# A hard-max attention kernel: an explicit order for its end phase, multiply-and-sum products, two pick steps at a time, and flag gathers beside value gathers

## Chip, cores and metric

The kernel runs on one core of one Trainium2 chip. The metric is device time in microseconds (us), lower is better. The profile's span, from the first to the last instruction, is about 2 us shorter than that time. Times below are medians of fast runs.

## The reference

For each query row, find the key with the largest dot product and return that key's value row.

```python
B, Sq, Sk, D = 4, 4096, 4096, 128          # q, k, v: float32, normal random
logits = np.matmul(q, k.transpose(0, 2, 1))
best = np.argmax(logits, axis=-1)
return v[b_idx, best, :].astype(np.float32)
```

## The kernel before

The queries form 128 tiles of 128 rows, 32 tiles a batch. The kernel screens keys in groups of four in half precision and repairs doubtful rows later:

- For each tile TensorE and ScalarE build upper bounds of the key groups. VectorE folds them into a table W (`fold`) and takes its eight best entries (`top`, MAX8 into TOP). This is the *screening loop*.
- For each tile GpSimd then fetches the best group's key differences with a *candidate gather* (kg). VectorE computes its half-precision dot products (`dots`), and for every chunk of tiles (8, towards the end 4, 2 and 1) a `pick` chooses the winning key. A *value gather* (vr) for each tile fetches the value rows, and the sync engine stores a chunk of tiles to the output.
- Rows whose decision was too close are *flagged*. For each half of the tiles up to 128 flagged rows are done again exactly: GpSimd gathers their record (FR), query (FQ), three key groups (FK) and, once VectorE has the exact products, the value (FV), and scatters FV over the output.

Picks, dots and the flag work are Python generators. A small scheduler advances them while the loop is written out, so what it decides is the fixed order of instructions on each engine.

```python
# pick (cut): one yield is one step of the scheduler
mx = tensor_reduce(d, max);              yield
lt = tensor_tensor(d, mx, is_lt);        yield
sel = lt * 2**20 + iota;                 yield
wi = tensor_reduce(sel, min);            yield
win = cand * 4 + wi
late_q += [value gather of each tile j] + [store of the chunk];  yield
near = (d + NEAR >= mx);                 yield
CNT = tensor_reduce(near, add)           # input of the flags
# exact (cut): for each of R = 3 key groups, 128 x 512 float32
pr = tensor_tensor(kk[:, r], qq, mult);  yield
d[:, r] = tensor_reduce(pr, add);        yield
# issue (cut), once a tile: one candidate gather, then flag gathers or value gathers
for _ in range(late):                    # late is 1 or 2
    (late_q if late_q and it > T + 1 else fast or late_q).pop(0)()
    while late_q and late_q[0] in stores:
        late_q.pop(0)()
# the loop (cut): loads for the next batch, its key differences, its transposes
if 2 <= qt < 10:    load_part(b + 1, qt - 2)       # keys
elif 10 <= qt < 18: load_part(b + 1, qt - 2)       # queries: natq, on GpSimd
if b + 1 < B and qt >= 13 and qt % 3 == 1:
    unit_q(b + 1, (qt - 13) // 3)                  # TensorE transposes natq
if it % NQT in (9, 13) and it < T:
    put_k(it // NQT + 1, it % NQT // 13)           # k<-kd, a 384 KB write on the sync queue
```

## Time and profile before

| | before |
|---|---|
| time | 494.8 us (494.76 to 495.12) |
| last MAX8 of the screening loop ends | 427.5 us |
| last candidate gather ends | 433.2 us |
| flag indices (rr) ready, FR issued | 445.6, 462.8 us |
| FV issued | 474.7 us |
| scatter issued to end | 477.7 to 478.7 us |
| span | 492.8 us |

The windows of the kernel before show busy time of each engine in three stretches. The columns after the engines are the granted share of the TensorE clock, the DMA share and GB/s:

```profile
core 0: us, PE busy (x) PEld busy (x) DVE busy (x) ACT busy (x) POOL busy (x), PEclk, DMA share, GB/s
40.00:427.00 387.00, 351.42 (x1748) 157.35 (x1746) 381.50 (x714) 364.61 (x460) 254.02 (x274) 1.00 0.38 90
427.00:479.00 52.00, 1.39 (x12) 1.22 (x12) 19.04 (x103) 0.00 (x0) 34.16 (x35) 0.50 0.33 94
479.00:493.00 14.00, 0.00 (x0) 0.00 (x0) 0.00 (x0) 0.00 (x0) 0.00 (x0) 0.50 0.01 4
```

In the first stretch VectorE (DVE) and ScalarE (ACT) are busy nearly all the time. In the second only GpSimd (POOL) works steadily. In the third nothing counts as busy.

The order of time in the tail of the kernel before, cut to the lines that mark it (start, duration, engine, instruction, and in brackets the idle time before it and what ended it):

```profile
426.24 1.22 DVE L229 MAX8 TOP<-W 128x8 f32<-128x1024 f32 x1
...
432.28 0.94 POOL L246 DMA_INDIRECT kg<-k,cand  x1 [0.30 <-DVE near L307]
...
445.40 0.16 DVE L407 SCALAR_TENSOR_TENSOR rr<-rr,rw 128x1 uint32<-128x1 uint32 x1
...
461.57 0.94 POOL L296 DMA_INDIRECT vr<-in_v_dram,win  x1 [0.30 <-issue]
...
462.82 1.01 POOL L411 DMA_INDIRECT FR<-rec,rr  x1 [0.30 <-issue]
464.14 1.00 POOL L411 DMA_INDIRECT FQ<-in_q_dram,row  x1 [0.30 <-issue]
...
465.92 1.00 POOL L411 DMA_INDIRECT FK<-in_k_dram,gb  x1 [0.78 <-DVE gb L425]
...
474.67 1.00 POOL L411 DMA_INDIRECT FV<-in_v_dram,xw_f  x1 [5.15 <-DVE xw_f L460]
477.69 1.02 POOL L433 DMA_INDIRECT out_dram<-FV,row  x1 [2.02 <-DMA FV<-in_v_dram,xw_f]
```

Nearly every value gather takes GpSimd 0.95 us and the next starts 0.30 us later, a pitch of 1.25 us. FR stands behind the last value gather although its index was ready 17 us earlier. Only FK, FV and the scatter wait for data.

Three more engines' lines of the kernel before matter later (I read them only after the result): the sync queue (SPq) near 150 us, the first query load of the next batch, and TensorE's first transpose of it.

```profile
147.57 0.33 SPq L74 DMA_DIRECT2D k<-kd  x1
...
151.85 0.60 POOL L65 DMA_DIRECT2D natq<-in_q_dram  x1
...
153.97 0.33 SPq L300 DMA_DIRECT2D out_dram<-vr  x1
154.41 0.38 SPq L314 DMA_DIRECT2D rec<-TOP  x1
...
154.84 0.29 PE L171 MATMUL uq<-identh,natq 128*128 128x128 f16 x2 [0.89 <-DMA natq<-in_q_dram]
```

The order is put (k<-kd), query load, output store, record write. TensorE waits 0.89 us for the load.

### The profile page before, as it was taken

How to read it: one execution, taken by the hardware profiler on the slowest of the kernel's cores; microseconds unless marked ns; L12 is line 12 of the kernel's file. 1: busy time of each engine (PE TensorE's matmuls, PEld its weight loads, DVE VectorE, ACT ScalarE, POOL GpSimd, SP SyncE). 2: the span in 40 equal slices, each digit the busy share in tenths (PEclk: the TensorE clock that was granted, in tenths of full speed). 3: DMA queues.
4: the chain of work that ended last, by engine and by line, in shares of the span. 5: the costliest groups of instructions: out<-in, count | busy, mean ns of one | idle time of the engine just before them, and what ended most of it. 6: DMA issues, size and time to landing. Idle time of an engine off the chain costs nothing. (4 is left out here: it accounts for less than half of the span.)

```text
span 492.8 us, 6520 instructions
## 1 busy us (share of the span) xinstructions
PE 385.1 (78%) x1960; PEld 174.6 (35%) x1960; DVE 419.6 (85%) x839; ACT 394.8 (80%) x498; POOL 305.7 (62%) x345
## 2 busy tenths in 40 slices
PE   6798999999999999999989989999988999010000
PEld 4344444444444444444444434444333333000000
DVE  3288999999999999999999989999999999781030
ACT  2999999999999999999999989999987999000000
POOL 9125445666788876667888755566646666677720
PEclk9999999999999999999999999999999999655555
DMA  8514452232557542325475412214213222233310
GB/s 141 127 30 83 82 105 57 55 99 55 128 95 167 122 120 57 102 55 124 94 167 122 123 46 86 62 51 124 68 49 92 54 68 85 68 112 112 94 48 0
DMA packets 25128, 43.48 MB, mean 88 GB/s; under 512 B 8040, under 2 KB 16875, under 8 KB 25088
## 3 DMA queue, kind: packets, MB, share of 16 engines
q0 software_dynamic: 18464, 30.97, 30.0%
q1 hardware_dynamic: 6624, 12.06, 6.7%
q8 instruction: 15, 0.25, 0.2%
q14 instruction: 25, 0.20, 0.1%
HBM read 39.59 MB, written 12.19 MB: 105 GB/s over the span
## 5 line engine op out<-in xcount | busy, mean ns | idle before, releaser
L200 ACT ACTIVATE A<-pd 128x1024 f16<-128x1024 f32 x256 | 263.1, 1032 | 12.0 <-PE pd L191 11.4
L246 POOL DMA_INDIRECT kg<-k,cand x128 | 124.3, 971 | 118.6 <-DVE p L265 31.5
L226 DVE TENSOR_TENSOR W<-psn,E 128x1024 int16<-128x1024 f32 x128 | 166.4, 1300 | 20.2 <-ACT E L213 12.4
L191 PE MATMUL psn<-kT,qT 128*128 128x512 f16 x512 | 151.9, 378 | 16.5 <-ACT A L200 10.7
L191 PE MATMUL pd<-kT,qT 128*128 128x512 f16 x512 | 152.2, 379 | 12.1 <-ACT A L200 11.1
L229 DVE MAX8 TOP<-W 128x8 f32<-128x1024 f32 x128 | 156.2, 1220 | 0.0
L210 PE MATMUL psn<-A,identh 128*128 128x512 f16 x512 | 152.1, 378 | 0.0
L296 POOL DMA_INDIRECT vr<-in_v_dram,win x128 | 127.6, 997 | 39.0 <-issue 37.5
L191 PEld LDWEIGHTS <-qT 128*128 128x128 f16 x1024 | 95.9, 97 | 148.5 <-issue 69.3
L213 ACT ACTIVATE E<-psn 128x1024 int16<-128x1024 f32 x128 | 131.0, 1024 | 1.3 <-PE psn L210 1.3
L210 PEld LDWEIGHTS <-identh 128*128 128x128 f16 x512 | 49.7, 97 | 60.8
L261 DVE TENSOR_TENSOR prod<-kg,natq 128x768 f16<-128x768 f16 (+1 forms) x65 | 35.2, 543 | 3.0 <-DMA kg<-k,cand 3.0
L173 ACT ACTIVATE qT<-uq 128x256 f16<-128x256 f32 x60 | 23.7, 394 | 1.1 <-PE uq L171 1.1
L265 DVE TENSOR_TENSOR p<-prod 128x384 f16<-128x384 f16 (+1 forms) x65 | 22.5, 349 | 0.0
L270 DVE TENSOR_REDUCE D<-p 128x6 f32<-128x192 f16 (+1 forms) x65 | 21.6, 334 | 0.0
L166 ACT ACTIVATE kT<-uk 128x256 f16<-128x256 f32 x48 | 18.9, 395 | 0.4 <-PE uk L163 0.4
L171 PE MATMUL uq<-identh,natq 128*128 128x128 f16 x120 | 16.5, 219 | 2.9 <-DMA natq<-in_q_dram 2.9
L351 PE MATMUL fp<-n,tri 128*128 128x1 f32 x4 | 0.9, 304 | 21.2 <-DVE n L343 21.2
L422 DVE TENSOR_SCALAR gi<-FR 128x3 uint32<-128x3 uint32 x2 | 0.3, 159 | 19.7 <-DMA FR<-rec,rr 19.7
L171 PEld LDWEIGHTS <-natq 128*128 128x128 f16 x120 | 11.3, 98 | 16.1 <-DMA natq<-in_q_dram 4.3
L62 POOL DMA_DIRECT2D natk<-in_k_dram x26 | 15.6, 602 | 0.9 <-POOLq L629 0.8
L162 PE MATMUL uk<-identh,natk 128*128 128x128 f16 x96 | 15.8, 219 | 0.0
(99 smaller groups left out, 191.6 us busy)
## 6 DMA issues: line engine op xcount, KB each, us to landing
out_dram<-vr SPq DMA_DIRECT2D x13, 512.0 KB, 2.8
k<-kd SPq DMA_DIRECT2D x8, 384.0 KB, 3.2
natk<-in_k_dram POOLq DMA_DIRECT2D x24, 128.0 KB, 3.8
natq<-in_q_dram POOLq DMA_DIRECT2D x24, 128.0 KB, 3.3
kg<-k,cand POOLq DMA_INDIRECT x128, 2.7
vr<-in_v_dram,win POOLq DMA_INDIRECT x128, 2.6
natk<-in_k_dram POOLq DMA_DIRECT2D x2, 512.0 KB, 5.1
out_dram<-vr SPq DMA_DIRECT2D x4, 256.0 KB, 2.1
```

Of the source, the lines that this page charges most:

```text
L171: nc.tensor.matmul(out=ps[:, i * P:(i + 1) * P], lhsT=natq[b % 2][:, g * 2 + i, :], rhs=identh, start=True, stop=True)
L173: nc.scalar.activation(out=qT[b % 2][:, g * 256:(g + 1) * 256], in_=ps, func=AF.Copy, scale=QSCALE)
L191: nc.tensor.matmul(out=ps[:, n * 512:(n + 1) * 512], lhsT=qT[b % 2][:, qt * P:(qt + 1) * P], rhs=kT[b % 2][:, u * 1024 + n * 512:u * 1024 ...
L200: nc.scalar.activation(out=A, in_=ps, func=AF.Abs)
L210: nc.tensor.matmul(out=ps[:, n * 512:(n + 1) * 512], lhsT=identh, rhs=A[:, n * 512:(n + 1) * 512], start=False, stop=True)
L213: nc.scalar.activation(out=E, in_=ps, func=AF.Relu)
L226: nc.vector.tensor_tensor(out=W_t[t % NW].bitcast(I16)[:, 1::2], in0=ps, in1=E, op=OP.max)
L229: nc.vector.max(out=TOP[:, t, :], in_=W_t[t % NW].bitcast(FP32))
L246: near_q.append(lambda j=j: nc.gpsimd.indirect_dma_start(out=kg[:, j].rearrange("p f d -> p (f d)"), out_offset=None, in_=k16[t0 // NQT], ...
L261: nc.vector.tensor_tensor(out=prod, in0=kg, in1=natq[b % 2][:, x - b * NQT:x - b * NQT + m, :].unsqueeze(2).to_broadcast([P, m, 3, P]), op ...
L265: nc.vector.tensor_tensor(out=p1, in0=prod[:, :, :, 0:64], in1=prod[:, :, :, 64:128], op=OP.add)
L296: late_q.append(lambda j=j: nc.gpsimd.indirect_dma_start(out=vr[:, j, :], out_offset=None, in_=v_flat, in_offset=IOA(ap=win[:, j:j + 1], a ...
```

## The change

Its intent: order the end phase by hand, so that the flag work of the second half starts early and its waits are filled with value gathers; compute the exact products with a multiply-and-sum instruction; stop flag gathers from displacing value gathers in the loop; and get winners, hence value gathers, earlier by taking two pick steps at a time.

```diff
 # pick: near and CNT come first
+        near = ...; yield
+        CNT = tensor_reduce(near, add); yield "cnt"
         lt = ...
 # exact
-            tensor_tensor(pr, kk[:, r], qq, mult)      # 128 x 512
-            tensor_reduce(d[:, r, :], pr, add)
+            for f in range(4):                         # 128 x 128
+                tensor_tensor_reduce(out=pr, in0=kk[:, r, f * P:(f + 1) * P], in1=qq,
+                                     op0=mult, op1=add, accum_out=d[:, r, f:f + 1])
 # chunks of tiles
-    cuts = list(range(0, T - 24 + 1, 8)) + [T - x for x in (20, 16, 12, 8, 6, 4, 2, 1, 0)]
+    cuts = list(range(0, T - 16 + 1, 8)) + [T - x for x in (12, 8, 4, 0)]
 # step: two pick steps at a time
-                else:
-                    moved |= advance(s, it, free)
+            elif advance(s, it, False) and s["kind"] == "pick" and s in live:
+                advance(s, it, False)
 # issue: a flag gather is added to the value gather
+        if fast and it >= rest[0]:
+            fast.pop(0)()
+            rest[0] = it + 3
+        take_late(2 if n == 0 and len(late_q) > 4 else 1)
 # end phase (new function flags_last, cut)
+        late(LATE)                                     # ten value gathers
+        get(FR, rec, rr); get(FQ, q_flat, row)
+        late(1)
+        for r in range(3): get(FK[:, r], k4, gb[:, r])
+        late(3)
+        win = whole(exact(FK, FQ, gb, 3, "fe"))
+        get(FV, v_flat, win)
+        late(1 << 20)                                  # the rest
+        scatter FV to out                              # waits for all stores
 ... (the loop rewritten for it in range(T), then an explicit drain of dots and picks)
```

More of the change, by code (lines that the diff above doesn't have):

```diff
@@ L23 @@
 NEAR = 0.5
+LATE = 10
 @with_exitstack
@@ L251, in gather @@
         near_q.append(mark)
-        start(dots(c, t0, n), "dots")
+        start(dots(c, t0, n), "dots", c)
     def dots(c, x, m):
@@ L281, in pick @@
         yield "dve",
+        near = sp.tile([P, n, 4], FP32, tag=f"near{n}", name=f"near_{c}")
+        nc.vector.scalar_tensor_tensor(out=near, in0=d, scalar=NEAR, in1=mx.to_broadcast([P, n, 4]),
+                                       op0=OP.add, op1=OP.is_ge)
+        yield "dve",
+        nc.vector.tensor_reduce(out=CNT[:, t0:t1], in_=near, axis=AX_X, op=OP.add)
+        done.add(("cnt", c))
+        yield "cnt",
         lt = sp.tile([P, n, 4], FP32, tag=f"lt{n}", name=f"lt_{c}")
@@ L293, in pick @@
         nc.vector.scalar_tensor_tensor(out=win, in0=cand, scalar=4.0, in1=wi, op0=OP.mult, op1=OP.add)
-        vr = rp.tile([P, n, P], FP32, tag=f"vr{n}", name=f"vr_{c}", bufs=3)
+        vr = rp.tile([P, n, P], FP32, tag=f"vr{n}", name=f"vr_{c}", bufs=3 if n == 8 else 4)
         for j in range(n):
@@ L304, in pick @@
         late_q.append(store)
-        yield "dve",
-        near = sp.tile([P, n, 4], FP32, tag=f"near{n}", name=f"near_{c}")
-        nc.vector.scalar_tensor_tensor(out=near, in0=d, scalar=NEAR, in1=mx.to_broadcast([P, n, 4]),
-                                       op0=OP.add, op1=OP.is_ge)
-        yield "dve",
-        nc.vector.tensor_reduce(out=CNT[:, t0:t1], in_=near, axis=AX_X, op=OP.add)
-        done.add(("cnt", c))
     def put_rec(t0, t1):
@@ L435, in flag_segment, with flags_first @@
         yield "until", lambda: not fast, 0
+    LF = {}
+    def flags_first(t0, t1):
+        S = t1 - t0
+        H = LF["H"] = fp.tile([P, S, 4], U32, tag="H", name="H_e")
+        nc.vector.tensor_scalar(out=H, in0=TOP.bitcast(U32)[:, t0:t1, 0:4], scalar1=16, scalar2=None,
+                                op0=OP.logical_shift_right)
+        F = LF["F"] = fp.tile([P, S], FP32, tag="F", name="F_e")
+        nc.vector.scalar_tensor_tensor(out=F, in0=H[:, :, 1], scalar=TAU, in1=H[:, :, 0], op0=OP.add, op1=OP.is_ge)
@@ new lines, in flags_last, with get @@
+    def flags_last(t0, t1, win_last, late):
+        S = t1 - t0
+        H, F = LF["H"], LF["F"]
+        nc.vector.scalar_tensor_tensor(out=F, in0=CNT[:, t0:t1], scalar=1.5, in1=F, op0=OP.is_gt, op1=OP.max)
+        Ec = fp.tile([P, S], FP32, tag="Ec", name="Ec_e")
+        nc.vector.tensor_tensor(out=Ec, in0=F, in1=codes[:, t0:t1], op=OP.mult)
+        e8 = fp.tile([P, 8], FP32, tag="e8", name="e8_e")
+        nc.vector.max(out=e8, in_=Ec)
+        val = fp.tile([P, 8], FP32, tag="val", name="val_e")
+        nc.vector.tensor_scalar(out=val, in0=e8, scalar1=0.5, scalar2=None, op0=OP.is_gt)
+        n2 = fp.tile([P, 3], FP32, tag="n2", name="n2_e")
+        nc.vector.tensor_reduce(out=n2[:, 0:1], in_=val, axis=AX_X, op=OP.add)
+        ps = pp.tile([P, 1024], FP32, tag="u", name="fp_e")
+        nc.tensor.matmul(out=ps[:, 0:1], lhsT=tri, rhs=n2[:, 0:1], start=True, stop=True)
+        win_last()
+        bs = fp.tile([P, 1], FP32, tag="bs", name="bs_e")
+        nc.vector.tensor_copy(out=bs, in_=ps[:, 0:1])
+        posn = fp.tile([P, 8], FP32, tag="posne", name="posn_e")
+        nc.vector.scalar_tensor_tensor(out=posn, in0=iota_r[:, 0:8], scalar=bs, in1=val, op0=OP.add, op1=OP.mult)
+        rec2 = fp.tile([P, 8, 2], BF16, tag="rec2", name="rec2_e")
+        nc.vector.tensor_copy(out=rec2[:, :, 0], in_=e8)
+        nc.vector.tensor_copy(out=rec2[:, :, 1], in_=iota_p.to_broadcast([P, 8]))
+        OH = fp.tile([P, 8, P], BF16, tag="OH", name="OH_e")
+        for z in range(8):
+            nc.vector.tensor_scalar(out=OH[:, z], in0=iota_h, scalar1=posn[:, z:z + 1], scalar2=None, op0=OP.is_equal)
+        ps2 = pp.tile([P, 1024], FP32, tag="u", name="fq_e")
+        for s in range(8):
+            nc.tensor.matmul(out=ps2[:, 0:2], lhsT=OH[:, s, :], rhs=rec2[:, s, :], start=s == 0, stop=s == 7)
+        nc.vector.tensor_reduce(out=n2[:, 1:2], in_=F, axis=AX_X, op=OP.add)
+        tp = fp.tile([P, 2], FP32, tag="tp", name="tp_e")
+        nc.vector.tensor_copy(out=tp, in_=ps2[:, 0:2])
+        rw = fp.tile([P, 2], FP32, tag="rw", name="rw_e")
+        nc.vector.tensor_scalar(out=rw[:, 0:1], in0=tp[:, 0:1], scalar1=0.5, scalar2=float(1 << 20), op0=OP.is_lt, op1=OP.mult)
+        rr = fp.tile([P, 1], U32, tag="rr", name="rr_e")
+        nc.vector.scalar_tensor_tensor(out=rr, in0=tp[:, 1:2], scalar=float(T), in1=tp[:, 0:1], op0=OP.mult, op1=OP.add)
+        nc.vector.scalar_tensor_tensor(out=rr, in0=rr, scalar=-1.0, in1=rw[:, 0:1], op0=OP.add, op1=OP.add)
+        tb = fp.tile([P, 2], U32, tag="tb", name="tb_e")
+        nc.vector.tensor_scalar(out=tb[:, 0:1], in0=tp[:, 0:1], scalar1=-1.0, scalar2=0.0, op0=OP.add, op1=OP.max)
+        nc.vector.scalar_tensor_tensor(out=rw[:, 1:2], in0=tp[:, 1:2], scalar=float(NQT), in1=tp[:, 0:1], op0=OP.mult, op1=OP.add)
+        nc.vector.tensor_scalar(out=tb[:, 1:2], in0=tb[:, 0:1], scalar1=NQT.bit_length() - 1, scalar2=None,
+                                op0=OP.logical_shift_right)
+        nc.vector.scalar_tensor_tensor(out=rw[:, 1:2], in0=tb[:, 1:2], scalar=float(Sq - NQT), in1=rw[:, 1:2], op0=OP.mult, op1=OP.add)
+        row = fp.tile([P, 1], U32, tag="row", name="row_e")
+        nc.vector.scalar_tensor_tensor(out=row, in0=rw[:, 1:2], scalar=-1.0, in1=rw[:, 0:1], op0=OP.add, op1=OP.add)
+        def get(dst, src, idx, hi):
+            nc.gpsimd.indirect_dma_start(out=dst, out_offset=None, in_=src, in_offset=IOA(ap=idx, axis=0),
+                                         bounds_check=hi - 1, oob_is_err=False)
+        late(LATE)
+        get(FR, rec, rr, P * T)
+        get(FQ, q_flat, row, P * T)
+        late(1)
+        bo = fp.tile([P, 1], U32, tag="bo", name="bo_e")
+        nc.vector.tensor_scalar(out=bo, in0=row, scalar1=Sq.bit_length() - 1, scalar2=NG.bit_length() - 1,
+                                op0=OP.logical_shift_right, op1=OP.logical_shift_left)
+        F4 = fp.tile([P, S], FP32, tag="F4", name="F4_e")
+        nc.vector.scalar_tensor_tensor(out=F4, in0=H[:, :, 3], scalar=TAU, in1=H[:, :, 0], op0=OP.add, op1=OP.is_ge)
+        nc.vector.tensor_reduce(out=n2[:, 2:3], in_=F4, axis=AX_X, op=OP.add)
+        nc.tensor.matmul(out=ps[:, 512:515], lhsT=ones, rhs=n2, start=True, stop=True)
+        gi = fp.tile([P, 3], U32, tag="gi", name="gi_e")
+        nc.vector.tensor_scalar(out=gi, in0=FR[:, 0:3], scalar1=NG - 1, scalar2=NG - 1, op0=OP.bitwise_and, op1=OP.bitwise_xor)
+        gb = fp.tile([P, 3], U32, tag="gb", name="gb_e")
+        nc.vector.tensor_tensor(out=gb, in0=gi, in1=bo.to_broadcast([P, 3]), op=OP.add)
+        for r in range(3):
+            get(FK[:, r, :], k4, gb[:, r:r + 1], B * NG)
+        tot = fp.tile([P, 3], FP32, tag="tot", name="tot_e")
+        nc.vector.tensor_copy(out=tot, in_=ps[:, 512:515])
+        hd = fp.tile([P, 2], FP32, tag="hd", name="hd_e")
+        nc.vector.tensor_scalar(out=hd[:, 0:1], in0=tot[:, 1:2], scalar1=-float(P), scalar2=0.0, op0=OP.add, op1=OP.max)
+        nc.vector.tensor_tensor(out=hd[:, 1:2], in0=tot[:, 1:2], in1=tot[:, 0:1], op=OP.subtract)
+        for a in (hd[:, 0:1], hd[:, 1:2], tot[:, 2:3]):
+            nc.vector.tensor_tensor(out=HARD, in0=HARD, in1=a, op=OP.add)
+        late(3)
+        win = whole(exact(FK, FQ, gb, 3, "fe"))
+        get(FV, v_flat, win, B * Sk)
+        late(1 << 20)
+        nc.gpsimd.indirect_dma_start(out=out_flat, out_offset=IOA(ap=row, axis=0), in_=FV, in_offset=None,
+                                     bounds_check=P * T - 1, oob_is_err=False)
@@ L439, in exact @@
         for r in range(R):
-            pr = fp.tile([P, 4, P], FP32, tag="xp", name=f"xp_{name}_{r}")
-            nc.vector.tensor_tensor(out=pr, in0=kk[:, r, :].rearrange("p (f d) -> p f d", f=4),
-                                    in1=qq.unsqueeze(1).to_broadcast([P, 4, P]), op=OP.mult)
-            yield "dve", 0.7
-            nc.vector.tensor_reduce(out=d[:, r, :], in_=pr, axis=AX_X, op=OP.add)
-            yield "dve", 0.7
+            for f in range(4):
+                pr = fp.tile([P, P], FP32, tag="xp", name=f"xp_{name}_{r}_{f}", bufs=2)
+                nc.vector.tensor_tensor_reduce(out=pr, in0=kk[:, r, f * P:(f + 1) * P], in1=qq, scale=1.0, scalar=0.0,
+                                               op0=OP.mult, op1=OP.add, accum_out=d[:, r, f:f + 1])
+                yield "dve", 0.2
         ix = fp.tile([P, R, 4], FP32, tag=f"xi{R}", name=f"xi_{name}")
@@ L508, with start @@
     live = []
-    def start(g, kind):
-        live.append({"g": g, "kind": kind, "wake": 0, "until": None, "n": 0})
+    def start(g, kind, c=None):
+        live.append({"g": g, "kind": kind, "c": c, "wake": 0, "until": None, "n": 0})
     def ready(s, it):
@@ L533, in advance @@
         return True
-    def step(it, free=False):
-        moved = True
-        while moved:
-            moved = False
-            waiting = [s for s in live if s["kind"] == "dots" and ready(s, it)]
-            quota = 2 if len(waiting) > 1 or free else 1
-            for s in list(live):
-                if s["kind"] == "dots":
-                    if quota and advance(s, it, free):
-                        quota -= 1
-                        moved = True
-                else:
-                    moved |= advance(s, it, free)
-            if not free:
-                return
@@ L551, in issue @@
-    def issue(it):
-        if it > T + 1:
-            while near_q:
-                near_q.pop(0)()
-            late = 2
-        else:
-            n = 0
-            while near_q and (n < 1 or near_q[0] in marks):
-                g = near_q.pop(0)
-                n += g not in marks
-                g()
-            late = 2 if n == 0 and len(late_q) + len(fast) > 4 else 1
-        for _ in range(late):
-            if fast or late_q:
-                (late_q if late_q and it > T + 1 else fast or late_q).pop(0)()
-            while late_q and late_q[0] in stores:
-                late_q.pop(0)()
@@ L569, with step @@
-    it = 0
-    while it < T + 2 or live or fast or near_q or late_q:
-        if it <= T:
-            b, qt = it // NQT, it % NQT
-            if 2 <= qt < 10:
-                load_part(b + 1, qt - 2)
-            elif 10 <= qt < 18:
-                load_part(b + 1, qt - 2)
-            if b + 1 < B and qt >= 8 and (qt - 8) % 3 < 2:
-                unit_k(b + 1, (qt - 8) // 3 * 2 + (qt - 8) % 3)
-            if b + 1 < B and qt >= 13 and qt % 3 == 1:
-                unit_q(b + 1, (qt - 13) // 3)
-            if 0 < it < 13:
-                unit_q(0, it + 3)
-            elif 0 < b < B and qt < 9:
-                unit_q(b, qt + 7)
-            if it > 0:
-                screen(it)
-        if 0 <= it - 1 < T:
+    def step(it):
+        waiting = [s for s in live if s["kind"] == "dots" and ready(s, it)]
+        quota = 2 if len(waiting) > 1 else 1
+        for s in list(live):
+            if s["kind"] == "dots":
+                if quota and advance(s, it, False):
+                    quota -= 1
+            elif advance(s, it, False) and s["kind"] == "pick" and s in live:
+                advance(s, it, False)
@@ new lines, with take_late @@
+    rest = [0]
+    def take_late(n):
+        while n > 0 and late_q:
+            g = late_q.pop(0)
+            n -= g not in stores
+            g()
+        while late_q and late_q[0] in stores:
+            late_q.pop(0)()
+    def issue(it):
+        n = 0
+        while near_q and (n < 1 or near_q[0] in marks):
+            g = near_q.pop(0)
+            n += g not in marks
+            g()
+        if fast and it >= rest[0]:
+            fast.pop(0)()
+            rest[0] = it + 3
+        take_late(2 if n == 0 and len(late_q) > 4 else 1)
@@ new lines, in gathers @@
+    def gathers(t):
+        for c, (t0, t1) in enumerate(chunks):
+            if t0 <= t < t1 and ((t - t0) % 2 or t == t1 - 1):
+                x = t0 + (t - t0) // 2 * 2
+                gather(c, x, t - x + 1)
+            if t == t0:
+                start(pick(c, t0, t1), "pick", c)
+        if t % 8 == 7:
+            put_rec(t - 7, t + 1)
+        if t == SEGS[1] - 1:
+            last = [c for c, x in enumerate(chunks) if x[1] == t + 1][0]
+            start(flag_segment(0, t + 1, lambda: ("cnt", last) in done, lambda: ("out", last) in done), "flags")
@@ new lines @@
+    for it in range(T):
+        b, qt = it // NQT, it % NQT
+        if 2 <= qt < 10:
+            load_part(b + 1, qt - 2)
+        elif 10 <= qt < 18:
+            load_part(b + 1, qt - 2)
+        if b + 1 < B and qt >= 8 and (qt - 8) % 3 < 2:
+            unit_k(b + 1, (qt - 8) // 3 * 2 + (qt - 8) % 3)
+        if b + 1 < B and qt >= 13 and qt % 3 == 1:
+            unit_q(b + 1, (qt - 13) // 3)
+        if 0 < it < 13:
+            unit_q(0, it + 3)
+        elif 0 < b < B and qt < 9:
+            unit_q(b, qt + 7)
+        if it > 0:
+            screen(it)
+        if it >= 1:
@@ L588 @@
             fold(it - 1)
-        if it % NQT in (9, 13) and it < T:
+        if it % NQT in (9, 13):
             put_k(it // NQT + 1, it % NQT // 13)
-        step(it, it >= T + 2)
-        if 0 <= it - 2 < T:
+        step(it)
+        if it >= 2:
             top(it - 2)
-        for t in ([it - 3] if it < T else [it - 3, it - 2] if it == T else [it - 2]):
-            if not 0 <= t < T:
-                continue
-            for c, (t0, t1) in enumerate(chunks):
-                if t0 <= t < t1 and ((t - t0) % 2 or t == t1 - 1):
-                    x = t0 + (t - t0) // 2 * 2
-                    gather(c, x, t - x + 1)
-                if t == t0:
-                    start(pick(c, t0, t1), "pick")
-            if t % 8 == 7:
-                put_rec(t - 7, t + 1)
-            for t0, t1 in zip(SEGS[:-1], SEGS[1:]):
-                if t == t1 - 1:
-                    last = [c for c, x in enumerate(chunks) if x[1] == t1][0]
-                    start(flag_segment(t0, t1, lambda last=last: ("cnt", last) in done,
-                                       lambda last=last: ("out", last) in done), "flags")
@@ L610, with flush, drain @@
-        step(it, it >= T + 2)
-        issue(it)
-        it += 1
+        if it >= 3:
+            gathers(it - 3)
+        step(it)
+        issue(it)
+    def flush():
+        while near_q:
+            near_q.pop(0)()
+    screen(T)
+    gathers(T - 3)
+    flush()
+    top(T - 2)
+    fold(T - 1)
+    top(T - 1)
+    gathers(T - 2)
+    gathers(T - 1)
+    flush()
+    assert not [s for s in live if s["kind"] == "flags"] and not fast
+    def drain(group, stop=None):
+        while group:
+            for s in list(group):
+                try:
+                    y = next(s["g"])
+                except StopIteration:
+                    group.remove(s)
+                    live.remove(s)
+                    continue
+                if y[0] == "until":
+                    assert y[1]()
+                if y[0] == stop:
+                    return
@@ L613 @@
+    for p in [s for s in live if s["kind"] == "pick"]:
+        c = p["c"]
+        dot = [s for s in live if s["kind"] == "dots" and s["c"] == c]
+        while dot:
+            two, dot = dot[:2], dot[2:]
+            drain(two)
+        last = c == len(chunks) - 1
+        if last:
+            flags_first(T // 2, T)
+        drain([p], "cnt" if last else None)
+    flags_last(T // 2, T, lambda: drain([p]), take_late)
     man.__exit__(None, None, None)
```

## The prediction

> **What bounds the kernel now.** The table of windows shows two phases. From 40 to 427 us VectorE is busy 94 to 100% (100% from 350 on), ScalarE nearly as much: the screening loop, about 3.02 us a query tile. From 427 on all matrix work is over, yet the span ends at 492.8. The order of time shows GpSimd alone there: after the last candidate gather (ends 433.2) it issues 23 value gathers at a pitch of 1.25 us, then FR, FQ, three FK, FV and the scatter, which ends at 478.7. Only the last seven wait: FK 0.8 us for the group numbers, FV 5.2 for the exact products, the scatter 2.0 for FV. The flag indices (rr, row) were ready at 445.6, yet FR came at 462.8: 17 us behind value gathers. From the scatter to the span's end are 14.1 us (the queue records show a GpSimd drain of 9.1); I take them as fixed.
>
> **What the change does.** GpSimd issues 322 transfers before and after. But in the loop flag gathers no longer displace value gathers, and the last chunks have 4 tiles instead of 2, 2, 1, 1, so 24 transfers (17 value, 7 flag) follow the last candidate gather, not 30: 6 x 1.25 = 7.5 us less. FR and FQ go after ten value gathers, FK one later, FV after three more, three are left behind FV: the waits of 0.8, 5.2 and 2.0 us are filled, some 7 us less. The last two candidate gathers go back to back, about 2 us sooner. New: the last store (128x512, 2.1 us to landing) comes after the last value gather and the scatter waits for it: about 4 us.
>
> Products: six 128x512 VectorE instructions of 0.69 us (4.4 us in the tail) become twelve multiply-and-sums of 128x128. The Trainium skill (VectorE: DVE Perf Modes, section "Two Vector instructions with no wait between them") says that an op that writes its accumulator out is two instructions; the build shows 24. Estimate from the trace (512 elements 0.69, one element 0.15 us, pitch 0.08 under the duration): 0.28 to 0.4 us a pair, about even in the loop; only the last group's four pairs, 1.2 us, follow the last FK landing.
>
> Cost: two pick steps at a time put dependent small instructions side by side (mx then near, sel then wi). Dependent neighbours in the tail have a pitch of 0.19 us, independent ones 0.07: 0.12 x 2 x 15 chunks, up to 3.6 us in a loop that VectorE bounds. Against it, about 1.8 us of picks and dots move behind the last top-8. Net: last top-8 at about 429, 1.4 us later.
>
> **Sum.** Candidate gathers end at 431.5, FR issues at 444 (rr just in time), FV at 456, the last value gather ends at 461, its store lands at 465, the scatter ends at 466: 12.5 us sooner. 494.8 - 12.5 = 482.3 us; range 479.5 to 485.5. Chances: faster 0.85, within 2% 0.14, slower 0.01.
>
> **What would show it.** Last candidate gather to scatter about 34 us, GpSimd idle little beyond its 0.3 us issue gaps, but for about 4 us before the scatter, released by the last store; no wait over 1 us before FV; the last top-8 ending between 428 and 430; 14 us after the scatter.
>
> **What would make it wrong.** Vector work after the last top-8 (8 tiles of dots, two picks, the flags) outlasting the ten gathers before FR, so FR stalls the queue; accumulator pairs of 0.5 us or more; dependent neighbours costing nothing, or more; three transfers in one tile delaying candidate gathers; a longer drain.

## The result

| | before | predicted | after |
|---|---|---|---|
| time, us | 494.8 | 482.3 (479.5 to 485.5) | 489.06 (488.84 to 489.34) |
| last MAX8 ends | 427.5 | 429 | 434.2 |
| last candidate gather ends | 433.2 | 431.5 | 437.6 |
| FR issued | 462.8 | 444 | 450.4 |
| FV issued | 474.7 | 456 | 462.6 |
| last value gather ends | 462.5 | 461 | 467.3 |
| scatter ends | 478.7 | 466 | 472.9 |
| scatter's end to end of span | 14.1 | 14.1 | 14.1 |

The ratio of after to before is 0.9883 (95% interval 0.9866 to 0.99): faster, but by less than 2%. Ratios here are the mean time of one kernel's fast runs over that of the other's of the same rounds, so not quite the ratio of the medians that I quote.

The windows of the changed kernel, cut at its own last MAX8 and at its scatter's end:

```profile
core 0: us, PE busy (x) PEld busy (x) DVE busy (x) ACT busy (x) POOL busy (x), PEclk, DMA share, GB/s
40.00:434.00 394.00, 354.51 (x1749) 158.34 (x1747) 382.35 (x718) 365.49 (x460) 259.37 (x282) 0.99 0.36 91
434.00:473.00 39.00, 2.28 (x12) 1.74 (x12) 18.58 (x109) 0.00 (x0) 26.30 (x27) 0.50 0.31 98
473.00:487.00 14.00, 0.00 (x0) 0.00 (x0) 0.00 (x0) 0.00 (x0) 0.00 (x0) 0.50 0.01 4
```

The second stretch shrank from 52 to 39 us, but the first grew from 387 to 394 us with no more VectorE work in it (381.5 and 382.4 us busy).

The tail of the changed kernel in the order of time:

```profile
432.93 1.23 DVE L230 MAX8 TOP<-W 128x8 f32<-128x1024 f32 x1
...
436.52 1.04 POOL L247 DMA_INDIRECT kg<-k,cand  x1 [0.30 <-issue]
...
447.41 0.16 DVE L483 SCALAR_TENSOR_TENSOR rr_e<-rr_e,rw_e 128x1 uint32<-128x1 uint32 x1
...
450.43 1.01 POOL L494 DMA_INDIRECT FR<-rec,rr_e  x1 [0.31 <-issue]
...
454.31 1.00 POOL L494 DMA_INDIRECT FK<-in_k_dram,gb_e  x1 [0.30 <-DVE HARD L520]
...
462.55 1.00 POOL L494 DMA_INDIRECT FV<-in_v_dram,xw_fe  x1 [0.67 <-DVE xw_fe L550]
```

Its last three lines, from a later window that shows the last store by itself:

```profile
466.35 0.94 POOL L304 DMA_INDIRECT vr<-in_v_dram,win  x1 [0.30 <-issue]
468.88 0.33 SPq L308 DMA_DIRECT2D out_dram<-vr  x1
471.86 1.01 POOL L525 DMA_INDIRECT out_dram<-FV,row_e  x1 [4.57 <-SPq L567]
```

FR follows its index (rr) after 2.9 us. FV waits 0.67 us. The scatter waits 4.57 us; the last store was issued 3.0 us before it. All this is near the forecast, only some 6 us late. So the loss is in the loop. Comparing the start of each MAX8 in the two traces shows where: at tile 42 the changed kernel is 0.4 us behind, at tile 43 it is 3.5 us behind, at tile 70 still 4.1, at tile 78 8.9 us, and 8.1 us at tile 124. (Parts of the jump near 78 are the first half's flag work, which stands at other tiles in the two kernels.)

The same engines near 150 us as shown of the kernel before:

```profile
151.10 0.33 SPq L308 DMA_DIRECT2D out_dram<-vr  x1
151.53 0.38 SPq L75 DMA_DIRECT2D k<-kd  x1
152.01 0.80 SPq L315 DMA_DIRECT2D rec<-TOP  x1
152.42 0.60 POOL L66 DMA_DIRECT2D natq<-in_q_dram  x1
...
157.24 0.28 PE L172 MATMUL uq<-identh,natq 128*128 128x128 f16 x2 [2.69 <-DMA natq<-in_q_dram]
```

The store is 2.9 us earlier and the put 4.0 us later, so that store, put and record write all go out within 1 us just ahead of the query load. TensorE now waits 2.69 us for the load. Then something else shows, in the windows of the changed kernel around that wait:

```profile
core 0: us, PE busy (x) PEld busy (x) DVE busy (x) ACT busy (x) POOL busy (x), PEclk, DMA share, GB/s
150.00:157.00 7.00, 4.04 (x21) 1.72 (x19) 7.00 (x11) 4.84 (x6) 5.77 (x7) 1.00 0.82 220
157.00:161.00 4.00, 3.76 (x12) 1.40 (x13) 1.91 (x5) 2.51 (x4) 3.09 (x5) 0.58 0.57 104
```

The same two windows of the kernel before:

```profile
150.00:157.00 7.00, 6.03 (x33) 2.65 (x31) 7.00 (x15) 6.36 (x9) 5.65 (x7) 1.00 0.76 168
157.00:161.00 4.00, 3.90 (x25) 1.90 (x24) 4.00 (x8) 4.00 (x6) 3.21 (x4) 1.00 0.72 129
```

From 157 to 161 us the granted clock is 0.58: the clock record has it halved from 157.6 us for 3.4 us, and again from 260.0 us for 3.4 us behind a wait of 2.77 us for the next batch's first query load. Before, it is 1.00 up to the end of the loop; VectorE is busy for all of the 4 us there, in the changed kernel for 1.91 of them.

Two pick steps at a time are why the store comes early: the winners of this chunk are known at 124.0 us instead of 124.8, so its first value gather still catches the slot at 124.8 (128.0 before), its eighth goes out at 147.5 instead of 150.8, and the store behind them comes as much sooner. The put stands behind the store in the sync queue, and so waits for the store's gathers although its data are there (VectorE finished kd at 148.0, the put went out at 151.5).

The Trainium skill (DMA: Bandwidth & Descriptors, section "Issuing engines are not separate DMA queues") says that transfers started by scalar, sync and GpSimd run on the same 16 DMA engines and interleave. The packet records agree that the engines are shared: in the kernel before the packets of that query load (1,024 bytes) start about 1.2 us after its issue; in the changed kernel they start about 2.3 us after it, behind the 4,096-byte packets of the store and most of the 3,072-byte packets of the put. They show little interleaving: the store's packets start from 151.9 to 153.6 us, the put's from 153.2, the load's from 154.7, mostly in the order of issue.

### The profile page after: what moved, and what is told of

Read it like the earlier page. It is cut to its first block, busy times and chain, and to the rows that moved or that the text cites. A ratio compares the mean times of both kernels' runs of the same rounds, so it can differ in the third digit from the quotient of the medians.

```text
span 487.0 us, 6530 instructions
## 1 busy us (share of the span) xinstructions
PE 389.1 (80%) x1960; PEld 176.1 (36%) x1960; DVE 421.0 (86%) x849; ACT 395.5 (81%) x498; POOL 302.3 (62%) x345
## 5 line engine op out<-in xcount | busy, mean ns | idle before, releaser
L192 PE MATMUL psn<-kT,qT 128*128 128x512 f16 x512 | 153.0, 380 | 18.0 <-ACT A L201 12.1
L211 PE MATMUL psn<-A,identh 128*128 128x512 f16 x512 | 153.0, 380 | 0.0
L304 POOL DMA_INDIRECT vr<-in_v_dram,win x128 | 124.1, 970 | 39.3 <-issue 35.6
L214 ACT ACTIVATE E<-psn 128x1024 int16<-128x1024 f32 x128 | 131.1, 1024 | 3.5 <-PE psn L211 3.5
L262 DVE TENSOR_TENSOR prod<-kg,natq 128x768 f16<-128x768 f16 x64 | 35.0, 549 | 0.0
L266 DVE TENSOR_TENSOR p<-prod 128x384 f16<-128x384 f16 x64 | 22.3, 351 | 0.0
L271 DVE TENSOR_REDUCE D<-p 128x6 f32<-128x192 f16 x64 | 21.5, 339 | 0.0
L269 DVE TENSOR_TENSOR p<-p 128x192 f16<-128x192 f16 x64 | 15.7, 248 | 0.0
L66 POOL DMA_DIRECT2D natq<-in_q_dram x26 | 15.5, 596 | 0.0
## 6 DMA issues: line engine op xcount, KB each, us to landing
natk<-in_k_dram POOLq DMA_DIRECT2D x24, 128.0 KB, 3.6
natq<-in_q_dram POOLq DMA_DIRECT2D x24, 128.0 KB, 3.1
```

Of the source, the lines that this page charges most:

```text
L192: nc.tensor.matmul(out=ps[:, n * 512:(n + 1) * 512], lhsT=qT[b % 2][:, qt * P:(qt + 1) * P], rhs=kT[b % 2][:, u * 1024 + n * 512:u * 1024 ...
L211: nc.tensor.matmul(out=ps[:, n * 512:(n + 1) * 512], lhsT=identh, rhs=A[:, n * 512:(n + 1) * 512], start=False, stop=True)
L214: nc.scalar.activation(out=E, in_=ps, func=AF.Relu)
L262: nc.vector.tensor_tensor(out=prod, in0=kg, in1=natq[b % 2][:, x - b * NQT:x - b * NQT + m, :].unsqueeze(2).to_broadcast([P, m, 3, P]), op ...
L266: nc.vector.tensor_tensor(out=p1, in0=prod[:, :, :, 0:64], in1=prod[:, :, :, 64:128], op=OP.add)
L304: late_q.append(lambda j=j: nc.gpsimd.indirect_dma_start(out=vr[:, j, :], out_offset=None, in_=v_flat, in_offset=IOA(ap=win[:, j:j + 1], a ...
```

## The experiments

Theory T: the pick change moves transfers so that the query load comes late, TensorE idles, and its clock is halved. Rival R: two dependent small instructions side by side cost VectorE time in every chunk. Rival F: flag gathers on top of value gathers overload GpSimd in the loop. The kernel before took 495.0 to 495.3 us beside all runs but two (d1_extra and b2_put_late, told last). The changed kernel was measured in other rounds, beside 494.8, so a difference to its 489.06 is uncertain by some 0.4 us.

### One pick step at a time (a1_single)

```diff
-            elif advance(s, it, False) and s["kind"] == "pick" and s in live:
-                advance(s, it, False)
+            else:
+                advance(s, it, False)
```

> The changed kernel with one pick step at a time again (as before), all else kept. Theory T (store order): two pick steps move an output store ahead of the k-difference put in the sync queue; store, put and record write then go out together with the first query load of the next batch, TensorE idles 2.7 us at its transposes twice, and its clock is halved for 3.4 us after each. T expects: in the sync queue the put comes before the store again, no TensorE wait over 1 us at those transposes, no clock drop before the loop ends, last top-8 ending at 427 to 429 instead of 434, time 482.5 to 485. Rival R (dependent neighbours cost VectorE about 0.12 us twice a chunk) also expects less, at most 3.6 us (485.5), gained evenly over the chunks. Rival F (flag gathers added to value gathers overload GpSimd) expects about 489.

483.39 us (ratio to before 0.9763, 0.9746 to 0.9779). Put, load, store are in the old order (147.6, 151.9, 156.7 us), no clock drop in the loop, the last MAX8 ends at 425.9 us, even earlier than I expected. The wait at the first transpose was 1.37 us, over the 1 us I had given. 26 transfers instead of 24 follow the last candidate gather. The loss comes with the pick change, but this run alone cannot tell T from R.

### The put one tile earlier (a2_put_early)

```diff
-        if it % NQT in (9, 13):
-            put_k(it // NQT + 1, it % NQT // 13)
+        if it % NQT in (8, 12):
+            put_k(it // NQT + 1, it % NQT // 12)
```

> The changed kernel with the two k-difference puts a batch one tile earlier, so that they stand before the output store in the sync queue; pick steps still two at a time. T expects the wait at the transposes to shrink below 1.5 us and no clock drop, 483 to 486 (the output store itself still falls near the query load). R and F expect no change, 488.5 to 489.5.

484.93 us (0.9789, 0.9772 to 0.9805). R and F fall short here: the picks are still double and the flag gathers still added. But the waits are 2.25 and 1.88 us, not below 1.5: the put was a small part of the delay. The clock was not halved at all. With no put ahead of it, the load's packets still start 2.4 us after its issue, behind the store's.

Why a wait of 2.25 us kept the clock where one of 2.69 lost it, can be worked out from the traces. Within each trace the changes of the clock record lie whole multiples of 3.41 us apart. Cut each trace into these steps, and add up in each the time in which TensorE neither multiplies nor loads weights. In all 14 traces, every one of the 1,699 full-clock steps with at most 1.88 us of such idle time was followed by a step at full clock, and each of the 24 with 1.91 us or more by one at half. The wait of 2.69 us lies in one step; a boundary cuts that of 2.25 us into 1.53 and 0.72 us. So the length of a wait alone does not decide; where it falls in the steps does too, and the steps lie differently in every run.

### The first transpose one tile later (a3_uq_late)

```diff
-        if b + 1 < B and qt >= 13 and qt % 3 == 1:
+        if b + 1 < B and (qt == 14 or qt >= 16 and qt % 3 == 1):
```

> The changed kernel with only the first query transpose of a batch moved one tile later, puts and stores as they are. T expects the collision of transfers to stay but TensorE not to wait for it: no wait over 1 us there, no clock drop, last top-8 ending at 427.5 to 429.5, time 482.5 to 484.5. R and F expect 488.5 to 489.5.

482.66 us (0.975, 0.9733 to 0.9766), as T expects. The waits are 0.51 us each, for ScalarE and not for the load; no clock drop, the last MAX8 ends at 427.8 us. Transfers stand as in the changed kernel; only TensorE's demand moved. The 6.4 us that separate this from 489.06 are what the two late loads cost.

### The pick change alone, in the kernel before (b1_double)

```diff
-                    moved |= advance(s, it, free)
+                    went = advance(s, it, free)
+                    moved |= went
+                    if went and not free and s["kind"] == "pick" and s in live:
+                        advance(s, it, free)
```

> The kernel before with the pick change alone (two steps at a time in the loop). T expects the same swap in the sync queue as in the changed kernel, waits of over 2 us at the transposes and clock drops near 157 and 260 us, and 498 to 502. R expects at most 3.6 us more, 496 to 498.5, spread evenly and without a clock drop. F expects 494.8.

502.4 us (1.0148, 1.0117 to 1.0179), so 7 us slower than before and 0.4 over T's range. Waits of 2.37 and 2.32 us; the clock was halved behind the first (156.9 us, for 3.4 us), not behind the second, which a step boundary cuts into 1.73 and 0.59 us. Of the two drops that I expected one came. The pick change by itself, without any of its partners, brings the loss. Not all of it is the two late loads: against the kernel before, MAX8 starts 4.3 us late at tile 66, after the first of them, 6.9 at tile 90, after the second, and 8.8 at the last tile. The last 1.9 us come where no late load stands; R may claim them (no run tests that by itself).

### Idle matmuls in front of the transpose (c1_filler)

```diff
+        if b > 0 and g == 0:
+            for i in range(8):
+                nc.tensor.matmul(out=ps, lhsT=wz[:, 0:P], rhs=wz[:, 0:256], start=True, stop=True)
```

> The changed kernel with eight idle matmuls of 256 columns put in front of each batch's first query transpose (their result is overwritten), so that TensorE is idle for a shorter time while it waits for the same late load; nothing moves in the transfer queues. Theory T2: about half of each loss is the halved clock[...] (drops seen behind 2.37, 2.69 and 2.77 us, none behind 2.25 and 2.32). T2 expects idle times below 2 us, no clock drop before the loop ends, and 485.5 to 487.5. Rival: the clock drop costs nothing because ScalarE and VectorE bind, the loss is the wait alone; 488.8 to 489.5.

486.52 us (0.9835, 0.9813 to 0.9856); the four runs are 485.55, 485.79, 487.25 and 487.88. In the profiled run TensorE's lines at the same place show the fillers, and then the transpose at nearly the same time as in the changed kernel (157.52 and 157.24 us), behind a shorter wait:

```profile
154.87 1.03 PE L173 MATMUL uq<-wz 128*128 128x256 f16 x8
157.52 0.28 PE L175 MATMUL uq<-identh,natq 128*128 128x128 f16 x2 [1.62 <-DMA natq<-in_q_dram]
```

Its windows show the clock at 1.00 where the changed kernel had 0.58:

```profile
core 0: us, PE busy (x) PEld busy (x) DVE busy (x) ACT busy (x) POOL busy (x), PEclk, DMA share, GB/s
150.00:157.00 7.00, 5.39 (x31) 2.69 (x29) 7.00 (x13) 5.27 (x7) 5.52 (x7) 1.00 0.85 222
157.00:161.00 4.00, 3.48 (x20) 1.71 (x21) 2.82 (x6) 3.05 (x4) 3.39 (x4) 1.00 0.61 107
```

There is no drop in its whole loop, and its last MAX8 ends 3.7 us earlier than in the changed kernel. The rival, a halved clock that costs nothing (488.8 to 489.5 us), falls. Of the 6.3 us by which a3_uq_late's last MAX8 is earlier, then, 3.7 us are the halved clock and the other 2.6 us the waits themselves, if the fillers cost nothing. This split rests on one profiled run, the fastest. The second idle time is 2.22 us, not below 2 as expected, but a step boundary cuts it in this run into 1.2 and 1.0 us. In the two runs that are 1.5 to 2.3 us slower the steps may have fallen otherwise and a drop have come; they were not profiled, so this is not shown.

### The old products (c2_old_products)

```diff
 # on a3_uq_late: exact() as in the kernel before
```

> The changed kernel with the late first query transpose (a3_uq_late, 482.66) and with the products of before (six 128x512 multiply or reduce instructions). In the traces a multiply-and-sum with its accumulator read has a pitch of 0.21 us (twelve: 2.5 us), an old instruction 0.6 in the loop (six: 3.7 us) and 0.72 in the tail (4.4 us). Expected: last top-8 1.2 us later than in a3_uq_late, the wait before FV from 1.0 to about 2 us, time 484 to 485.5. If the new products gain nothing: 482.7.

484.87 us (0.979, 0.9774 to 0.9806): 2.2 us more than a3_uq_late, as expected. The last MAX8 ends 1.05 us later and the wait before FV is 2.14 instead of 0.95 us. The new products in the tail of the changed kernel look like this:

```profile
457.73 0.29 DVE L533 CUSTOM_DVE_ANT_0 xp_fe<-FK,FQ 128x128 f32<-128x128 f32 x1 [3.19 <-DMA FK<-in_k_dram,gb_e]
457.95 0.08 DVE L533 DVE_READ_ACCUMULATOR2_ANT xd_fe<- 128x1 f32 x1
457.95 0.28 DVE L533 CUSTOM_DVE_ANT_0 xp_fe<-FK,FQ 128x128 f32<-128x128 f32 x1
458.16 0.08 DVE L533 DVE_READ_ACCUMULATOR2_ANT xd_fe<- 128x1 f32 x1
```

A pair of multiply-and-sum and accumulator read has a pitch of 0.21 us, below my estimate of 0.28 to 0.4.

### Flag gathers displacing value gathers again (c3_displace)

```diff
 # on a3_uq_late, in issue() (cut: the lines that these replace):
+        room = 2 if n == 0 and len(late_q) + len(fast) > 4 else 1
+        while fast and room:
+            fast.pop(0)()
+            room -= 1
+        take_late(room)
```

> a3_uq_late (482.66) with the first half's flag gathers displacing value gathers again, as before. The built order then has 31 transfers behind the last candidate gather instead of 24, the seven more all value gathers behind FV. Expected 7 x 1.25 = 8.75 us more, 490.5 to 492; the end of the loop unchanged within 0.5 us. If the extra transfers in the loop cost time there (rival F), the loop ends earlier by 1 us or more and the sum is below 490.

491.08 us (0.9917, 0.9901 to 0.9934): 8.4 us more than a3_uq_late for seven more transfers in the tail, 1.2 us each; expected were 8.75. The last MAX8 ends at 427.6 us against 427.8: the added transfers cost the loop nothing. F is out.

### All value gathers ahead of FV (c4_tail)

```diff
 # on a3_uq_late
-        late(3)
         win = whole(exact(FK, FQ, gb, 3, "fe"))
-        get(FV, v_flat, win, B * Sk)
         late(1 << 20)
+        get(FV, v_flat, win, B * Sk)
```

> a3_uq_late (482.66) with all value gathers issued before FV, so that the last store runs while FV lands. Expected: the gap before the scatter from 4.5 to about 2 us, no wait before FV, 480 to 481. If the scatter's wait is not for the last store: 482.7.

481.45 us (0.9719, 0.9703 to 0.9735). FV does not wait, but the gap before the scatter is 3.98 us, not 2:

```profile
458.43 0.94 POOL L304 DMA_INDIRECT vr<-in_v_dram,win  x1 [0.30 <-issue]
459.68 1.01 POOL L494 DMA_INDIRECT FV<-in_v_dram,xw_fe  x1 [0.30 <-DVEq L566]
...
464.67 1.01 POOL L524 DMA_INDIRECT out_dram<-FV,row_e  x1 [3.98 <-SPq L566]
```

From the end of the last value gather to the scatter are 5.3 us (4.5 in a3_uq_late): its landing, the store and the store's landing are one chain, and the landing of FV hides only part of it. The gain is 1.2 us instead of about 2, and the time lies 0.45 us over the 480 to 481 expected. This version beats both kernels.

### The query loads one tile earlier (e1_load_first)

```diff
-        elif 10 <= qt < 18:
-            load_part(b + 1, qt - 2)
+        if 9 <= qt < 17:
+            load_part(b + 1, qt - 1)
```

> The changed kernel with the query loads of the next batch issued one tile earlier, so that the first of them is issued about 2.5 us sooner, ahead of the output store that the change moved in front of it; the transposes stay where they are. Theory T, as sharpened by the put runs (what counts is whether the 512 KB output store goes out before or behind the first query load; the put adds little): no wait over 1.4 us at the first transposes, no clock drop before the loop ends, 482.5 to 484.5. If the late load has another cause than the store in front of it, 487 to 489.

482.62 us (0.9751, 0.9735 to 0.9767), as T expects. The load now goes out ahead of the store:

```profile
149.25 0.64 POOL L66 DMA_DIRECT2D natq<-in_q_dram  x1
...
150.92 0.33 SPq L308 DMA_DIRECT2D out_dram<-vr  x1
151.35 0.38 SPq L75 DMA_DIRECT2D k<-kd  x1
151.83 0.50 SPq L315 DMA_DIRECT2D rec<-TOP  x1
```

TensorE's trace has no wait over 0.3 us at these transposes and no clock drop. Together with a3_uq_late this settles the cause: it is enough to move either the load or its use by a tile.

### The put one tile later, in the kernel before (b2_put_late)

```diff
-        if it % NQT in (9, 13) and it < T:
-            put_k(it // NQT + 1, it % NQT // 13)
+        if it % NQT in (10, 14) and it < T:
+            put_k(it // NQT + 1, it % NQT // 14)
```

> The kernel before with the k-difference puts one tile later and nothing else: in the built sync queue the output store now stands ahead of the put, as in the changed kernel, but pick steps stay single and no dependent instructions are neighbours. T (the order of store and put, and the late query load that follows) expects waits of over 1.5 us at the first query transpose of batches 2 and 3, [...]and 497 to 501. R (dependent neighbours) expects 494.8 to 495.5.

507.7 us, on a chip where the kernel before took 505 to 512 us (0.997, 0.9894 to 1.0046): the time decides nothing. The trace does: the store was ahead of the put, but the query load (151.4 us) was ahead of both (153.0 and 153.4), and the waits were 0.58 and 0.50 us. My expectation was wrong: the order of store and put is not what counts, but that of store and load. With a2_put_early this is why I restated T before e1_load_first.

### A second value gather late in the loop (d1_extra, d1_extra_again)

```diff
 # on c4_tail
-LATE = 10
+LATE = 8
-        take_late(2 if n == 0 and len(late_q) > 4 else 1)
+        take_late(2 if n == 0 and len(late_q) > 4 or it >= T - 24 and it % 2 == 0 else 1)
```

> c4_tail (481.45) with a second value gather in every other one of the last 24 tiles, and FR after eight value gathers instead of ten. The built order has 21 transfers behind the last candidate gather instead of 24: 3 x 1.25 = 3.75 us less, if the loop does not pay for it. Expected 477 to 478.5, last top-8 within 0.5 us of c4_tail. If three transfers a tile delay the candidate gathers in the loop: last top-8 over 1 us later and 479 or more.

519.92 us on the same disturbed chip as b2_put_late (1.0186, 1.0106 to 1.0267). In its trace the engines stand still for several us with no releaser in the profile, in many places of the loop. I draw nothing from it and ran the same kernel again:

> d1_extra once more: its first run fell on a chip where the kernel before itself took 505 to 512 us. Expected as then, on a chip where the kernel before takes about 495: 477 to 478.5 with the last top-8 within 0.5 us of c4_tail's 427.9 if the extra transfers cost the loop nothing; 479 or more if they delay its candidate gathers. The vector chain to the flag indices may now be what FR waits for (in c4_tail they came 2.9 us ahead of FR).

481.6 us (0.9724, 0.9707 to 0.974), level with c4_tail. Three fewer transfers follow the last candidate gather, and the last MAX8 is unmoved (427.8 us), but that gather now ends at 434.9 us instead of 431.3: GpSimd issues without a break there, so the extra gathers only changed places with the candidate gathers. No gain, a miss. Why d1_extra was so much slower than the kernel before on that chip stays open.

## Why the prediction was wrong

Wrong in size: the forecast was 12.5 us of gain, measured were 5.7.

- **The step that failed** is "Net: last top-8 at about 429, 1.4 us later." It measured 6.7 us later (427.5 to 434.2). I had costed only the instructions that move on VectorE. Left out was what the pick change does to the transfers: the output store moved from behind to ahead of the next batch's first query load. That delayed the load, TensorE idled 2.7 us twice, and its clock was halved for 3.4 us each time. Taking the demand away (a3_uq_late) or the collision (e1_load_first) gives back 6.4 us of time each; some 3.7 us of it is the clock (c1_filler, one profiled run). The order of the sync queue could have been read from the build before predicting; I had read only VectorE, GpSimd and the end of the sync queue. With this put right, the result is 482.6 us against the 482.3 predicted, so the other terms together hold. That they come so close is partly luck: in a3_uq_late the last MAX8 ends 1.2 us earlier than forecast (427.8 against 429) and the last candidate gather 0.9 us later behind it than forecast.
- **Dependent neighbours** ("up to 3.6 us in a loop that VectorE bounds"): at the last MAX8 a1_single is 1.1 us ahead of e1_load_first and 1.9 ahead of a3_uq_late, with other small things moved as well. The last 1.9 us of b1_double fit that. About 2 us at most, so over-sized. At tile 98 a1_single and e1_load_first are level (336.3 us), so it does not come evenly over the chunks; why is not shown.
- **Transfers in the tail** ("6 x 1.25 = 7.5 us less", "some 7 us" of filled waits): right. The stretch from the last candidate gather's end to the scatter is 34.3 us, predicted 34; GpSimd's only gaps there over 0.4 us are 0.67 before FV and 4.57 before the scatter. c3_displace shows the price of a transfer, 1.2 us.
- **The last two candidate gathers** ("back to back, about 2 us sooner"): they were back to back, but behind two others that came just before, so the last ended 3.4 us after the last MAX8, where I had 2.5.
- **The scatter's wait** ("about 4 us"): 4.57 us.
- **Products** ("about even in the loop"): better than that. A pair costs 0.21 us, the loop gains 1.05 us, the whole kernel 2.2 (c2_old_products).
- **FR stalled by vector work**: it did not happen; rr was ready 2.9 us ahead of FR, with 0.3 us between gathers there.
- **14 us after the scatter**: 14.09.

## What to carry to other kernels

A change of order on one engine also moves the stores and loads that hang on it: before pricing it, read the built order of the DMA-issuing queues and look for bursts that now stand in front of a small load which someone will wait for. A wait of TensorE of 2 to 3 us can cost the loop more through the clock than directly (here some 3.7 us for two halvings, beside 2.6 us for the two waits), and where it falls in the steps of the clock record decides too: of b1_double's waits of 2.37 and 2.32 us only the first cost it the clock. So give loads that TensorE waits for a tile of slack, or move their use a tile later. In a tail that one queue serves at a fixed pitch, count the transfers behind the last dependent one: each costs a pitch (here 1.25 us), and a wait in that queue is hidden only as far as other transfers stand in it.

## What the Trainium skill lacked or had wrong

- TensorE: Matmul & The Clock Gate, section "HAM oscillation — how this bites in real kernels", gives the rule of no TensorE idle gaps over about 3.4 us. Here idle gaps of 2.37, 2.69 and 2.77 us were each followed by a halved clock, and gaps of 2.32, 2.25, 2.22 and 1.88 us were not; in the start-up of c3_displace one of 1.53 us was (at 11.8 us). The measurement decides: 3.4 us of idle time is not needed, and the length of a gap is not the rule. What parts the cases in all 14 traces is the idle time summed over one 3.41 us step of the clock record: at most 1.88 us kept the clock, 1.91 us or more halved it. Behind each wait of 2.37 us or more at these transposes the halved clock lasted 3.4 us, which agrees with the length of the window that the page gives in its section "What's actually happening".
- DMA: Bandwidth & Descriptors, section "Issuing engines are not separate DMA queues", says that transfers interleave. Near 153 us of the changed kernel the packets of store, put and load went out mostly one after the other, in the order of issue. I found no figure there for how late a small load comes behind a burst: a 128 KB load issued 1.3 us behind a 512 KB store and 0.9 us behind a 384 KB put released its user 4.8 us after issue instead of 3.0.
- The same page, section "Anatomy of one DMA — SWDGE (gpsimd) path", calls descriptor generation small. I found no figure there for the pitch of gathers issued back to back. Here a gather by 128 row indices kept GpSimd busy for 0.95 us with 0.30 us to the next, and that pitch set the length of the tail; how much of it is descriptor generation, no run shows.
- VectorE: DVE Perf Modes, section "Two Vector instructions with no wait between them", says that an op with an accumulator output is two instructions, which the trace confirms. I found no cost for the pair there; it measured 0.29 us for 128 float32 elements and 0.08 us for the read, at a pitch of 0.21 us for both.
